# Products, differences and small sums of one transformer layer: from GpSimd to VectorE, and some sums a few matmuls later

## The chip, the cores and the metric

The kernel runs on one core of a Trainium2 chip. A core has five engines with a queue of instructions each, which they work off in order: TensorE (PE, matmuls, with its weight loads shown apart as PEld), VectorE (DVE), ScalarE (ACT), GpSimd (POOL) and SyncE (SP, which here only starts DMAs). The metric is device time in microseconds for one execution. Before the change it is 1555.61 us, the median of three runs (1555.39 to 1558.89).

## The reference, cut to what matters

The reference is one step of a one-layer streaming encoder: 1024 prompt frames and 8 short sequences of 16 frames, 1152 columns in all, model width 1024. A conditioning vector gives shifts, scales and gates for every sub-layer (adaLN). Half of the heads are a gated linear recurrence (HGRN2), the other half a latent attention (MLA) with rotary keys.

```python
def trunk_layer(x, c, pos, w, cache_lat, cache_kpe, st_hg, st_conv):
    mod = (jax.nn.silu(c) @ w_ada + b_ada)[:, None, :]
    sh1, sc1, g1, sh2, sc2, g2 = jnp.split(mod, 6, axis=-1)
    h = rmsnorm(x, g_mix) * (1.0 + sc1) + sh1
    proj = h @ w_in
    hq, hf, hi, hg, hcq, hckv, hkpe = jnp.split(proj, points, axis=-1)
    o_hg, st_hg_new = hgrn_mixer(hq, hf, hi, hg, lb, hg_g, st_hg)
    o_mla, lat_new, kpe_new = mla_mixer(hcq, hckv, hkpe, pos, ...)
    x = x + g1 * (jnp.concatenate([o_hg, o_mla], axis=-1) @ w_out)
    h2 = rmsnorm(x, g_ffn) * (1.0 + sc2) + sh2
    f, conv_new = conv_glu(h2, w_up, conv_w, conv_b, w_down, st_conv)
    return x + g2 * f, ...
```

The parts that the change touches are `h @ w_in`, the recurrence (`o` of a head is normalised with `rsqrt(mean(o * o))` and multiplied with a gain and `silu(hg)`), the rotary embedding (`x1 * cos - x2 * sin`, `x2 * cos + x1 * sin`) and the queries `rmsnorm(hcq) @ w_uq`.

## The kernel before, in words

Activations lie transposed: 128 features on the partitions, 1152 frames along the free axis, so that 1024 features are 8 tiles. A matmul in full precision is made of three: each operand is split into a rounded high part and the rest (`hi`, `lo`; `hh` and `hl` for the normalised input), and `mm3` (L291 to L295) issues hi by hi, hi by lo and lo by hi. A split is always a copy on ScalarE that rounds (`hi`), and then a subtraction of two SBUF tiles (`lo`).

The part of the program with the changed instructions goes as follows. `front` (0 to about 98 us) loads the input, makes the conditioning of the first sub-layer, normalises, and projects the first head's gates and values. Its order on TensorE, VectorE and ScalarE is the order of the code; all behind it is ordered by a scheduler, which simulates the engines with a table of costs and places each instruction on its engine's queue in the order in which it expects it to be ready. Then `phase_b` makes, for each of four heads, three units. A unit is 128 output features; `unit` (L612) runs three groups of 384 columns, and a group is 24 matmuls of 128x384 into one PSUM bank (`mm`, four banks in turn), which ScalarE copies out (L626). The weights of a unit come through `wload` (L272): DMA, high part on ScalarE (L283), low part (L284). `mla_in` (L914) goes on in the same way with five units for the latent queries and keys and one for the rotary key, and from about 430 us with the query up-projection, whose groups are 9 matmuls long; here ScalarE and then VectorE (L974, `ql`) read the PSUM bank before it is free again. Keys, scores and values of the attention follow until about 670 us, and the output projection and the channel mixer behind that; the last of the changed instructions (L905) ends at 490.6 us.

Everything else in that part is written as generators that run between the groups of main matmuls. After each group `step(n)` moves each background generator on by n pieces, and each slow one by two:

```python
    def step(self, n):
        for _ in range(n):
            self.advance(self.bg)
        for _ in range(2):
            self.advance(self.slow)
```

A piece ends at a `yield`. So a `yield` more sets what follows it behind more of the main matmuls in the program. The generators are these:
- `hgrn` (L645), the recurrence of one head: forget gate `f` and key `k` (L657, L659), seven levels of running sums and products `X` (L670 to L720) with small matmuls in L701 and L708, the products of the chunks, the state, and the output `ot`. The output is squared and split (`sq`, `sh`, `sl`, L798 to L800), summed over the partitions by matmuls with a matrix of ones (L806 for `sh`, L807 for `sl`), turned into a reciprocal root by five instructions (`rstd`, L298 to L303), and multiplied with the gate (L810, L811). With n = 4 a head's three units give it 36 pieces; the fourth head has 27 (three units with n = 3) before it is drained.
- `ada_rest` (L411), slow: the rest of the conditioning. Per pair of blocks it loads weights `wa`, multiplies (L381), copies the partial sums to SBUF on ScalarE (L390), and after a `yield` adds them up by two matmuls with a selection matrix (L394), which VectorE reads.
- In `mla_in`: `latent_q` and `latent_kv` (normalising, L833), `rope` (L850: rotated copy `rq` by DMA, products with `cos` and `sin` in L858 and L859, sum in L864), and `rope_q` (L896: splits in L903 and L905).

Names in rows: `w` are weight tiles, `X`, `Sa`, `Pa`, `k`, `f` tiles of the recurrence, `po` the outputs of units, `qr` rotary queries, `rq` their rotated copies, `u` the split up-projections of keys and values (L953, L954), `bg` PSUM banks of the background work, `s` and `t` small tiles, `c` constants.

Of the kernel before, what the change touches and what calls it, by code (L numbers as in the profile page):

```python
# [197 lines left out]
class Layer:  # L198
# [73 lines left out]
    def wload(self, src, shape, eng=None, new=None):  # L272
        nc = self.nc
        w = new or self.w
        raw, hi, lo = w(shape), w(shape, F32R), w(shape, F32R)
        nc.sync.dma_start(raw, src)
        if eng == "both":
            with self.tc.high_priority():
                nc.scalar.copy(hi, raw)
                nc.vector.tensor_sub(lo[:, :7], raw[:, :7], hi[:, :7].bitcast(F32))  # L280
                nc.gpsimd.tensor_sub(lo[:, 7:], raw[:, 7:], hi[:, 7:].bitcast(F32))
            return hi, lo
        nc.scalar.copy(hi, raw)  # L283
        (eng or nc.gpsimd).tensor_sub(lo, raw, hi.bitcast(F32))  # L284
        return hi, lo
# [100 lines left out]
    def ada_out(self, part, bs):  # L386
        nc = self.nc
        n = len(bs)
        sb = self.s([P, 256])
        nc.scalar.copy(sb, part[:, :256])  # L390
        yield
        res = self.ps("bg")
        for j in range(2):
            nc.tensor.matmul(res[:, 9 * n * j:9 * n * (j + 1)], lhsT=sb[:, P * j:P * j + P], rhs=self.sel[:, :9 * n], start=True, stop=True)  # L394
        for q, b in enumerate(bs):
            for j, (m, i) in enumerate(ADA_BLOCKS[b]):
                bias = self.vec[:, V_BADA + 8 * m + i:V_BADA + 8 * m + i + 1]
                o = self.mod[:, m, i]
                r = res[:, 9 * (n * j + q):9 * (n * j + q) + 9]
                if m in (SC1, SC2):  # L400
                    g = (V_GMIX if m == SC1 else V_GFFN) + i
                    nc.vector.tensor_scalar(o, r, bias, self.vec[:, g:g + 1], op0=ALU.add, op1=ALU.mult)
                else:
                    nc.vector.tensor_scalar_add(o, r, bias)
        yield
# [29 lines left out]
    def front(self):  # L435
# [21 lines left out]
        def stats(g):  # L457
# [3 lines left out]
            for kt in range(KT):  # L461
                if g == 0:
                    sq = l if kt == KT - 1 else self.s([P, TG])
                    nc.scalar.activation(sq, xs[kt][:, c], AF.Square)
                    if kt % 2:
                        nc.vector.tensor_add(sq, sq, pair)
                        nc.tensor.matmul(p[:, :TG], lhsT=self.ones, rhs=sq, start=kt == 1, stop=kt == KT - 1)
                    pair = sq
                else:
                    self.sumsq(l, xs[kt][:, c], kt == 0, nc.vector if g == 1 else nc.gpsimd)  # L470
                    yield
# [48 lines left out]
        with self.tc.manual_schedule(engines={mybir.EngineType.PE, mybir.EngineType.Activation, mybir.EngineType.DVE}):  # L520
# [4 lines left out]
            next(ad)  # L525
            W[0][1](nc.gpsimd, lambda: prep(0, 0))
            W[1][1](nc.vector)
            banks += [self.ps("mm") for _ in range(4)] + [self.ps("bg") for _ in range(2)]
            for kt in range(KT):
# [29 lines left out]
                if kt < 3:  # L559
                    W[kt + 2][1](nc.gpsimd if kt == 0 else nc.vector)  # L560
                if kt >= 2:
# [87 lines left out]
    def hgrn(self, hd, hf, hg, hq, v):  # L649
# [19 lines left out]
        for li, h in enumerate(LEVELS + (32,)):  # L669
# [3 lines left out]
            else:  # L673
                X = self.b(s="X")

                def vw(a, i):
                    return a[:, :ns].rearrange("p (n two h) -> p n two h", two=2, h=h)[:, :, i]
# [9 lines left out]
                if h == 1:  # L687
                    nc.gpsimd.tensor_copy(vw(X, 0), vw(k, 0))
                    nc.vector.tensor_mul(vw(X, 1), vw(hq, 1), vw(f, 1))
# [35 lines left out]
        nc.vector.tensor_mul(X[:, :, 0], X[:, :, 0], half(k, 0))  # L725
        nc.gpsimd.tensor_mul(X[:, :, 1], X[:, :, 1], half(hq, 1))
        tf = half(Pa, 0)[:, :, 63:64].to_broadcast([P, 8, 64])
# [35 lines left out]
        vb = self.b([P, 4, P], s="vb")  # L763
        nc.gpsimd.tensor_mul(vb, v[:, 8:9].to_broadcast([P, 4, P]), self.of4.unsqueeze(2).to_broadcast([P, 4, P]))
        sn = self.b([P, NB, P], s="sn")
        dec = Pa[:, SEQ:].rearrange("p (b t) -> p b t", t=DS)[:, :, DS - 1:DS].to_broadcast([P, NB, P])
        nc.gpsimd.tensor_mul(sn, s0, dec)
        pu = [self.ps("bg") for _ in range(2)]
# [17 lines left out]
        for o in range(0, NT, 4):  # L786
# [13 lines left out]
            nc.vector.tensor_sub(sl[:, c], sq[:, c], sh[:, c].bitcast(F32))  # L800
            yield
        vv, r = self.b(s="vv"), self.b(s="r")
        for o in range(0, T, TG):
# [5 lines left out]
        self.rstd(r, vv, sq)  # L809
        nc.gpsimd.tensor_mul(gate, gate, ot)  # L810
        nc.vector.tensor_mul(ot, gate, r)  # L811
# [38 lines left out]
    def rope(self, t, new):  # L850
# [6 lines left out]
        yield  # L857
        nc.gpsimd.tensor_mul(t, t, self.cos)  # L858
        nc.gpsimd.tensor_mul(q, q, self.sin)  # L859
        yield  # L860
# [34 lines left out]
    def rope_q(self, h, rr, new):  # L895
# [4 lines left out]
        a, b = self.u([P, SEQ], F32R, s="qs"), self.u([P, SEQ], F32R, s="qs")  # L900
        eng = nc.gpsimd if h else nc.vector
        nc.scalar.copy(a[:64], rr[:64, :SEQ])
# [10 lines left out]
    def mla_in(self):  # L913
# [24 lines left out]
        for n, u in enumerate(order):  # L938
            if n % 2 == 0:
# [4 lines left out]
                nc.scalar.copy(hi, raw)  # L944
                nc.gpsimd.tensor_sub(lo, raw, hi.bitcast(F32))
                for i, j in enumerate(pr):
# [280 lines left out]
    def sumsq(self, acc, x, first, eng=None):  # L1227
        nc = self.nc
        eng = eng or nc.gpsimd
        if first:  # L1230
# [424 lines left out]
```

## Time and profile before

| | |
|---|---|
| Median of three runs | 1555.61 us |
| The profiled execution's own time | 1556.36 us |
| Its span | 1554.5 us |
| Mean granted clock of TensorE | 0.983 |
| PE busy | 1489.3 us, 96% |
| DVE busy | 974.1 us, 63% |
| ACT busy | 690.5 us, 44% |
| POOL busy | 225.7 us, 15% |

The span begins with the first instruction that the profiler records and ends with the last; the execution's own time is 1.86 us longer. An engine is busy from the start of an instruction to its end, also where it is held up inside it. Rows of waits say which engine and line waited for which, how long in total, how often, and the longest; rows of the timeline say when an instruction began and how long it, or several merged ones (x3), took. The granted clock of TensorE is 1.00 at 2.4 GHz and 0.50 at 1.2 GHz.

### The profile page before, as it was taken

The numbers are of one execution on the slowest core, as the hardware profiler recorded it, in microseconds if no ns is written. First come the engines' busy times: TensorE is split into PE (matmuls) and PEld (weight loads), VectorE is DVE, ScalarE is ACT, GpSimd is POOL, SyncE is SP. The second block draws the span as 40 slices with busy tenths as digits, with TensorE's granted clock in tenths as the row PEclk, the third lists the DMA queues.
The fourth block names the chain that finished last, engine by engine and source line by source line (L and its number), as shares of the span: only waits on it lengthen the run. The fifth ranks groups of instructions, "written<-read, shape, count | busy, mean of one in ns | idle before, by whom it ended". The sixth has DMA issues, their size and how long they took to land.

```text
span 1554.5 us, 28456 instructions
## 1 busy us (share of the span) xinstructions
PE 1489.3 (96%) x11756; PEld 1386.5 (89%) x11756; DVE 974.1 (63%) x1540; ACT 690.5 (44%) x1231; POOL 225.7 (15%) x217
## 2 busy tenths in 40 slices
PE   6999999999999999998699999999999999999997
PEld 4897778998998978698699999999999999999997
DVE  5677667476777656358776655665666554473384
ACT  4453435263546646336554443443444443343352
POOL 1122232333242000012300000000000000000020
PEclk8999999999999999999899999999999999999999
DMA  9234622112131356744112211221122288455360
GB/s 345 87 109 141 217 89 106 43 72 74 50 93 26 109 192 213 285 162 165 56 56 72 85 70 67 77 85 71 58 85 83 72 279 294 154 177 199 102 250 29
DMA packets 71922, 194.42 MB, mean 125 GB/s; under 512 B 8112, under 2 KB 30384, under 8 KB 71792
## 3 DMA queue, kind: packets, MB, share of 16 engines
q1 hardware_dynamic: 60624, 165.62, 30.8%
q10 hardware_dynamic: 11168, 26.98, 4.5%
q8 instruction: 92, 1.51, 0.4%
q14 instruction: 38, 0.31, 0.1%
HBM read 159.63 MB, written 31.17 MB: 123 GB/s over the span
## 4 chain that ended last, share of the span: by engine, by line
PE 85%; DVE 7%; ACT 3%; issue 2%; DMA 2%; POOL 1%; SPq 0%; ACTq 0%; DVEq 0%; POOLq 0%
PE mm L1453 18%; PE bg L1453 13%; PE mm L293 11%; PE mm L294 11%; PE mm L295 11%; PE bg L294 3%; PE bg L295 3%; PE bg L293 3%; PE bg L1139 2%; PE bg L381 1%; PE bg L708 1%; PE bg L1182 1%; DVE sl L800 1%; DMA wa<-in_w_ada 1%; PE bg L791 1%
## 5 line engine op out<-in xcount | busy, mean ns | idle before, releaser
L1453 PE MATMUL mm<-U,W 128*128 128x288 f32 x1848 | 260.8, 296 | 11.5 <-ACT U L288 9.6
L1453 PEld LDWEIGHTS mm<-U,W 128*128 128x128 f32 x1848 | 251.5, 189 | 13.3 <-ACT U L288 9.8
L1453 PE MATMUL bg<-U,W 128*128 128x288 f32 x1320 | 189.3, 297 | 0.0
L1453 PEld LDWEIGHTS bg<-U,W 128*128 128x128 f32 x1320 | 181.7, 190 | 0.3
L289 DVE TENSOR_TENSOR W<-B,W 128x512 fp32r<-128x512 f32 (+1 forms) x132 | 102.5, 780 | 106.7 <-ACT W L288 104.5
L288 ACT CAST W<-B 128x512 fp32r<-128x512 f32 (+1 forms) x132 | 91.0, 692 | 144.8 <-issue 46.8
L293 PE MATMUL mm<-hh,w 128*128 128x384 f32 x432 | 152.7, 353 | 0.0
L294 PE MATMUL mm<-hl,w 128*128 128x384 f32 x432 | 149.5, 346 | 2.0 <-DVE hl L486 2.0
L295 PE MATMUL mm<-hh,w 128*128 128x384 f32 x432 | 149.0, 345 | 0.0
L289 DVE TENSOR_TENSOR U<-W,U 128x1024 fp32r<-128x1024 f32 (+2 forms) x66 | 74.9, 1167 | 70.4 <-ACT U L288 70.3
L288 ACT CAST U<-W 128x1024 fp32r<-128x1024 f32 (+2 forms) x66 | 61.7, 972 | 87.8 <-PE mm L294 74.5
L293 PEld LDWEIGHTS mm<-hh,w 128*128 128x128 f32 x432 | 83.1, 192 | 8.2 <-issue 7.4
L293 PE MATMUL bg<-U,U 128*128 128x448 f32 (+1 forms) x264 | 90.0, 341 | 0.2 <-DVE B L1461 0.2
L294 PE MATMUL mm<-U,U 128*128 128x448 f32 (+1 forms) x264 | 89.2, 338 | 0.0
L293 PE MATMUL mm<-U,U 128*128 128x448 f32 (+1 forms) x264 | 89.2, 338 | 0.0
L295 PE MATMUL mm<-U,U 128*128 128x448 f32 (+1 forms) x264 | 89.2, 338 | 0.0
L295 PE MATMUL bg<-U,U 128*128 128x448 f32 (+1 forms) x264 | 89.2, 338 | 0.0
L294 PE MATMUL bg<-U,U 128*128 128x448 f32 (+1 forms) x264 | 89.2, 338 | 0.0
L1456 ACT COPY B<-mm 128x288 f32<-128x288 f32 x132 | 51.8, 393 | 82.0 <-PE mm L1453 66.0
L294 PEld LDWEIGHTS mm<-hl,w 128*128 128x128 f32 x432 | 83.4, 193 | 3.5 <-DVE hl L486 2.3
L295 PEld LDWEIGHTS mm<-hh,w 128*128 128x128 f32 x432 | 83.3, 193 | 0.8 <-issue 0.8
L293 PE MATMUL mm<-mh,W 128*128 128x288 f32 x256 | 77.0, 302 | 5.5 <-DVE x L1372 3.4
(405 smaller groups left out, 3343.8 us busy)
## 6 DMA issues: line engine op xcount, KB each, us to landing
wa<-in_w_ada SPq DMA_DIRECT2D x48, 512.0 KB, 6.9
B<-in_w_up SPq DMA_DIRECT2D x44, 512.0 KB, 3.2
W<-in_w_down SPq DMA_DIRECT2D x44, 512.0 KB, 4.6
gd<-B ACTq DMA_DIRECT2D x22, 576.0 KB, 2.8
B<-in_w_down SPq DMA_DIRECT2D x22, 512.0 KB, 3.3
w<-in_w_in SPq DMA_DIRECT2D x18, 512.0 KB, 3.5
lT<-in_latT SPq DMA_DIRECT2D x16, 512.0 KB, 8.0
ln<-in_lat SPq DMA_DIRECT2D x16, 512.0 KB, 6.0
```

The source lines that it names most:

```text
L288: self.nc.scalar.copy(hi, raw)
L289: self.nc.vector.tensor_sub(lo, raw, hi.bitcast(F32))
L293: mm(out, lhsT=w[0], rhs=x[0], start=start, stop=False)
L294: mm(out, lhsT=w[0], rhs=x[1], start=False, stop=False)
L295: mm(out, lhsT=w[1], rhs=x[0], start=False, stop=stop)
L381: self.nc.tensor.matmul(part[32 * j:32 * j + 32, :256], lhsT=sc[:, 4 * half + j], rhs=w[half][:, j], start=first and half == 0, stop=last ...
L708: nc.tensor.matmul(pb[c:c + 32, 32 * j:32 * j + 32], lhsT=xl[:, o:o + 32], rhs=xr[:, o:o + 32], start=True, stop=True, tile_position=(0, c))
L791: nc.tensor.matmul(pb[:, c], lhsT=v[:, j], rhs=AF_[:, j], start=True, stop=j == 0)
L800: nc.vector.tensor_sub(sl[:, c], sq[:, c], sh[:, c].bitcast(F32))
L1139: mm(d[64 * j:64 * j + 64, :w], lhsT=q, rhs=ks[j][c], start=c == 0, stop=c == 2, tile_position=(0, 64 * j))
L1453: nc.tensor.matmul(out, lhsT=l[:, k], rhs=x[:, k], start=start and k == 0 and i == 0, stop=stop and k == 3 and i == 2, skip_group_check=True)
L1456: nc.scalar.copy(t[:, h], X[h][:, :HALF])
```

## The change

Fourteen kinds of instructions change their engine, and two places get more `yield`s.

From GpSimd to VectorE go: the low part of the unit weights (L284, 17 of 128x1024) and of two weights in `front` (L454), the sums of squares over the third group of columns (L470 and L1235, 7 of 128x384), one product `X` of each head (L726, 128x512), `vb` and `sn` of each head (L764 128x512, L767 128x1024), the gate product of each head (L810, 128x1152), both rotary products (L858 and L859, 6 of 128x1152), the splits of two rotary queries (L903, L905, 2 of 64x1024), and the low part of the query up-projection weights (L945, 3 of 128x768). One copy per head (L688, 128x576) goes from GpSimd to ScalarE. The matmuls of the sums L806 and L807 come three pieces later, and those of L394 one piece later when they are for two blocks. GpSimd keeps 157 of 214 rows of its program, VectorE has 1541 in place of 1481; TensorE has the same matmuls. Lines from L394 on have numbers higher by 2 after the change, those from L806 on by 4.

```diff
--- before.py
+++ after.py
@@ -281,7 +281,7 @@
                 nc.gpsimd.tensor_sub(lo[:, 7:], raw[:, 7:], hi[:, 7:].bitcast(F32))
             return hi, lo
         nc.scalar.copy(hi, raw)
-        (eng or nc.gpsimd).tensor_sub(lo, raw, hi.bitcast(F32))
+        nc.vector.tensor_sub(lo, raw, hi.bitcast(F32))
         return hi, lo
 
     def split(self, hi, lo, raw):
@@ -389,6 +389,8 @@
         sb = self.s([P, 256])
         nc.scalar.copy(sb, part[:, :256])
         yield
+        if len(bs) > 1:
+            yield
         res = self.ps("bg")
         for j in range(2):
             nc.tensor.matmul(res[:, 9 * n * j:9 * n * (j + 1)], lhsT=sb[:, P * j:P * j + P], rhs=self.sel[:, :9 * n], start=True, stop=True)
@@ -467,7 +469,7 @@
                         nc.tensor.matmul(p[:, :TG], lhsT=self.ones, rhs=sq, start=kt == 1, stop=kt == KT - 1)
                     pair = sq
                 else:
-                    self.sumsq(l, xs[kt][:, c], kt == 0, nc.vector if g == 1 else nc.gpsimd)
+                    self.sumsq(l, xs[kt][:, c], kt == 0, nc.vector)
                     yield
             if g:
                 nc.tensor.matmul(p[:, :TG], lhsT=self.ones, rhs=l, start=True, stop=True)
@@ -523,7 +525,7 @@
             ad = self.ada(0, wa[0])
             next(ad)
             next(ad)
-            W[0][1](nc.gpsimd, lambda: prep(0, 0))
+            W[0][1](nc.vector, lambda: prep(0, 0))
             W[1][1](nc.vector)
             banks += [self.ps("mm") for _ in range(4)] + [self.ps("bg") for _ in range(2)]
             for kt in range(KT):
@@ -557,7 +559,7 @@
                 if kt + 1 < KT:
                     prep(kt + 1, 0)
                 if kt < 3:
-                    W[kt + 2][1](nc.gpsimd if kt == 0 else nc.vector)
+                    W[kt + 2][1](nc.vector)
                 if kt >= 2:
                     for _ in range(4):
                         next(early, 0)
@@ -685,7 +687,7 @@
                 nc.vector.tensor_add(vw(Sa, 0), vw(Sa, 0), ts)
                 nc.vector.tensor_add(vw(Pa, 1), vw(Pa, 1), tf)
                 if h == 1:
-                    nc.gpsimd.tensor_copy(vw(X, 0), vw(k, 0))
+                    nc.scalar.copy(vw(X, 0), vw(k, 0))
                     nc.vector.tensor_mul(vw(X, 1), vw(hq, 1), vw(f, 1))
                 else:
                     nc.vector.tensor_mul(vw(X, 0), vw(X, 0), vw(k, 0))
@@ -723,7 +725,7 @@
         nc.scalar.activation(X[:, :, 0], half(Sa, 0), AF.Exp)
         nc.scalar.activation(X[:, :, 1], half(Pa, 1), AF.Exp)
         nc.vector.tensor_mul(X[:, :, 0], X[:, :, 0], half(k, 0))
-        nc.gpsimd.tensor_mul(X[:, :, 1], X[:, :, 1], half(hq, 1))
+        nc.vector.tensor_mul(X[:, :, 1], X[:, :, 1], half(hq, 1))
         tf = half(Pa, 0)[:, :, 63:64].to_broadcast([P, 8, 64])
         ts = half(Pa, 1)[:, :, 63:64].to_broadcast([P, 8, 64])
         nc.vector.tensor_add(half(Sa, 0), half(Sa, 0), ts)
@@ -761,10 +763,10 @@
                     nc.vector.scalar_tensor_tensor(S[:, j], S[:, j - 1], Pa[:, P * j + P - 1:P * j + P], u, op0=ALU.mult, op1=ALU.add)
         nc.scalar.dma_start(self.O["sp_o"][hd], S[:, 7])
         vb = self.b([P, 4, P], s="vb")
-        nc.gpsimd.tensor_mul(vb, v[:, 8:9].to_broadcast([P, 4, P]), self.of4.unsqueeze(2).to_broadcast([P, 4, P]))
+        nc.vector.tensor_mul(vb, v[:, 8:9].to_broadcast([P, 4, P]), self.of4.unsqueeze(2).to_broadcast([P, 4, P]))
         sn = self.b([P, NB, P], s="sn")
         dec = Pa[:, SEQ:].rearrange("p (b t) -> p b t", t=DS)[:, :, DS - 1:DS].to_broadcast([P, NB, P])
-        nc.gpsimd.tensor_mul(sn, s0, dec)
+        nc.vector.tensor_mul(sn, s0, dec)
         pu = [self.ps("bg") for _ in range(2)]
         for i in range(2):
             c = slice(64 * i, 64 * i + 64)
@@ -799,6 +801,8 @@
             nc.scalar.copy(sh[:, c], sq[:, c])
             nc.vector.tensor_sub(sl[:, c], sq[:, c], sh[:, c].bitcast(F32))
             yield
+        for _ in range(3):
+            yield
         vv, r = self.b(s="vv"), self.b(s="r")
         for o in range(0, T, TG):
             c = slice(o, o + TG)
@@ -807,7 +811,7 @@
             nc.tensor.matmul(p, lhsT=self.ones_r, rhs=sl[:, c], start=False, stop=True)
             nc.vector.tensor_scalar(vv[:, c], p, 1.0 / P, EPS, op0=ALU.mult, op1=ALU.add)
         self.rstd(r, vv, sq)
-        nc.gpsimd.tensor_mul(gate, gate, ot)
+        nc.vector.tensor_mul(gate, gate, ot)
         nc.vector.tensor_mul(ot, gate, r)
         nc.scalar.dma_start(self.mix[hd], ot)
         yield
@@ -855,8 +859,8 @@
             nc.sync.dma_start(q[d:d + 32], t[e:e + 32])
         yield
         yield
-        nc.gpsimd.tensor_mul(t, t, self.cos)
-        nc.gpsimd.tensor_mul(q, q, self.sin)
+        nc.vector.tensor_mul(t, t, self.cos)
+        nc.vector.tensor_mul(q, q, self.sin)
         yield
         yield
         yield
@@ -898,7 +902,7 @@
         yield
         yield
         a, b = self.u([P, SEQ], F32R, s="qs"), self.u([P, SEQ], F32R, s="qs")
-        eng = nc.gpsimd if h else nc.vector
+        eng = nc.vector
         nc.scalar.copy(a[:64], rr[:64, :SEQ])
         eng.tensor_sub(a[64:], rr[:64, :SEQ], a[:64].bitcast(F32))
         nc.scalar.copy(b[64:], rr[64:, :SEQ])
@@ -942,7 +946,7 @@
                 for i, j in enumerate(pr):
                     nc.sync.dma_start(raw[:, i], I["w_uq"][:, j])
                 nc.scalar.copy(hi, raw)
-                nc.gpsimd.tensor_sub(lo, raw, hi.bitcast(F32))
+                nc.vector.tensor_sub(lo, raw, hi.bitcast(F32))
                 for i, j in enumerate(pr):
                     wq[j] = (hi[:, i], lo[:, i])
             if n == 3:
@@ -1226,7 +1230,7 @@
 
     def sumsq(self, acc, x, first, eng=None):
         nc = self.nc
-        eng = eng or nc.gpsimd
+        eng = eng or nc.vector
         if first:
             nc.scalar.activation(acc, x, AF.Square)
         else:
```

The scheduler then orders all queues anew, and three places of its result are shown here.

On TensorE, in the group of main matmuls in which the third head's output is summed (`mm` are the main matmuls, `bg` the sums of `sh` and `sl`), before the change:

```order
L806 MATMUL bg_3579<-sh_3539,c_76 128x384
L294 MATMUL mm_3602<-hl_113,w_2986 128x384
L806 MATMUL bg_3583<-sh_3539,c_76 128x384
L295 MATMUL mm_3602<-hh_112,w_2987 128x384
L807 MATMUL bg_3579<-sl_3540,c_76 128x384
L807 MATMUL bg_3583<-sl_3540,c_76 128x384
L293 MATMUL mm_3602<-hh_114,w_2986 128x384
```

and after it (L810 and L811 are the former L806 and L807):

```order
L295 MATMUL mm_3580<-hh_122,w_2987 128x384
L810 MATMUL bg_3608<-sh_3539,c_76 128x384
L811 MATMUL bg_3608<-sl_3540,c_76 128x384
L810 MATMUL bg_3612<-sh_3539,c_76 128x384
L811 MATMUL bg_3612<-sl_3540,c_76 128x384
L810 MATMUL bg_3616<-sh_3539,c_76 128x384
L811 MATMUL bg_3616<-sl_3540,c_76 128x384
L293 MATMUL mm_3628<-hh_108,w_2986 128x384
```

All six sums now stand together behind the whole group of 24 main matmuls, where before they began ahead of it, right behind the products of the head's output.

On TensorE, in the second head, where the sums of the conditioning (L394) stand among the main matmuls and the small matmuls of the levels (L708), before:

```order
L708 MATMUL bg_2184<-X_2177 32x32 x36
L708 MATMUL bg_2229<-X_2222 32x32 x36
L381 MATMUL bg_2138<-wa_2147,c_74 32x256 x4
L381 MATMUL bg_2138<-wa_2148,c_74 32x256 x4
L293 MATMUL mm_2291<-hh_108,w_1779 128x384
L294 MATMUL mm_2291<-hl_109,w_1779 128x384
L295 MATMUL mm_2291<-hh_108,w_1780 128x384
L293 MATMUL mm_2291<-hh_110,w_1779 128x384
L394 MATMUL bg_2277<-c_70,s_2275 128x18 x2
L294 MATMUL mm_2291<-hl_111,w_1779 128x384
```

and after:

```order
L381 MATMUL bg_2104<-wa_2113,c_74 32x256 x4
L381 MATMUL bg_2104<-wa_2114,c_74 32x256 x4
L293 MATMUL mm_2250<-hh_108,w_1740 128x384
L294 MATMUL mm_2250<-hl_109,w_1740 128x384
L295 MATMUL mm_2250<-hh_108,w_1741 128x384
L293 MATMUL mm_2250<-hh_110,w_1740 128x384
L294 MATMUL mm_2250<-hl_111,w_1740 128x384
L295 MATMUL mm_2250<-hh_110,w_1741 128x384
L710 MATMUL bg_2195<-X_2188 32x32 x36
L293 MATMUL mm_2250<-hh_112,w_1740 128x384
```

The sum that belongs to these two rows of L381 stood four main matmuls behind them; it now stands 32 behind them, with L710 (the former L708) of two levels and L703 of the next in between. The L708 of a head, which stood in pairs, stand apart among the main matmuls.

On VectorE, in the query up-projection, before the change (L974 are the subtractions that free the PSUM bank `mm` named in them):

```order
L974 TENSOR_TENSOR ql_4798<-mm_4812,qh_4797 128x384
L954 TENSOR_TENSOR u_4845<-w_4843,u_4844 128x1024
L974 TENSOR_TENSOR ql_4798<-mm_4830,qh_4797 128x256
L954 TENSOR_TENSOR u_4851<-w_4849,u_4850 128x1024
L864 TENSOR_TENSOR po_4581<-po_4581,rq_4715 128x1152
L974 TENSOR_TENSOR ql_4856<-mm_4857,qh_4855 128x384
L974 TENSOR_TENSOR ql_4856<-mm_4870,qh_4855 128x384
L974 TENSOR_TENSOR ql_4856<-mm_4882,qh_4855 128x256
L289 TENSOR_TENSOR kl_4826<-po_4581,kh_4825 128x1024
L974 TENSOR_TENSOR ql_4903<-mm_4904,qh_4902 128x384
L974 TENSOR_TENSOR ql_4903<-mm_4926,qh_4902 128x384
L864 TENSOR_TENSOR qr_4703<-qr_4703,rq_4758 128x1152
```

and after (L978, L958, L868 are the former L974, L954, L864, and L862 and L863 the rotary products):

```order
L978 TENSOR_TENSOR ql_4798<-mm_4812,qh_4797 128x384
L862 TENSOR_TENSOR po_4581<-po_4581,cos_4376 128x1152
L863 TENSOR_TENSOR rq_4715<-rq_4715,sin_4377 128x1152
L978 TENSOR_TENSOR ql_4798<-mm_4830,qh_4797 128x256
L868 TENSOR_TENSOR po_4581<-po_4581,rq_4715 128x1152
L958 TENSOR_TENSOR u_4845<-w_4843,u_4844 128x1024
L958 TENSOR_TENSOR u_4851<-w_4849,u_4850 128x1024
L862 TENSOR_TENSOR qr_4703<-qr_4703,cos_4376 128x1152
L863 TENSOR_TENSOR rq_4758<-rq_4758,sin_4377 128x1152
L289 TENSOR_TENSOR kl_4826<-po_4581,kh_4825 128x1024
L978 TENSOR_TENSOR ql_4856<-mm_4857,qh_4855 128x384
L868 TENSOR_TENSOR qr_4703<-qr_4703,rq_4758 128x1152
```

Between the subtraction on `mm_4812` and the one on `mm_4857` stood four instructions; nine stand there now, four of them rotary products, and one the split of the rotary key (L289).

## Rows read from the trace of the kernel before

**Rows 1.** Busy time by stretch: stretch, its length, busy us of each engine, clock, DMA.

```profile
0.00:60.00 60.00, 45.58 (x303) 33.19 (x304) 36.52 (x76) 28.23 (x56) 11.46 (x13) 0.87 0.75 278
60.00:215.00 155.00, 148.44 (x1875) 131.81 (x1874) 106.41 (x197) 71.66 (x130) 40.02 (x23) 0.97 0.40 135
215.00:545.00 330.00, 316.87 (x2889) 292.84 (x2890) 223.00 (x366) 157.73 (x321) 88.80 (x48) 0.99 0.21 70
545.00:1554.00 1009.00, 978.39 (x6693) 928.63 (x6689) 608.15 (x902) 432.83 (x725) 85.41 (x135) 0.99 0.38 133
```

**Rows 2.** Waits of TensorE, whole span: total us, times, longest us.

```profile
PE bg L807 <- DVE sl L800: 5.9, 4, 1.6
PE bg L394 <- ACT s L390: 5.3, 6, 2.0
...
PE mm L1047 <- ACT w L1024: 3.4, 2, 3.1
PE mm L293 <- DVE ql L974: 3.1, 1, 3.1
...
PE mm L294 <- DVE hl L486: 2.0, 1, 2.0
...
PE bg L311 <- DVE acc L840: 1.1, 1, 1.1
PE bg L701 <- DVE X L692: 1.1, 1, 1.1
PE bg L708 <- DVE k L659: 1.0, 1, 1.0
```

**Rows 3.** Waits of TensorE from 0 to 60 us, those of L394 alone.

```profile
PE bg L394 <- ACT s L390: 2.0, 4, 0.5
```

**Rows 4.** Busy time in three stretches at half clock (columns as in Rows 1).

```profile
57.80:61.20 3.40, 3.28 (x11) 3.28 (x12) 3.40 (x5) 1.76 (x4) 2.13 (x2) 0.50 0.00 0
201.20:208.00 6.80, 6.67 (x22) 6.67 (x23) 6.05 (x12) 1.33 (x3) 2.75 (x1) 0.50 0.80 272
457.20:460.60 3.40, 3.40 (x13) 3.40 (x11) 2.90 (x5) 2.06 (x5) 1.64 (x1) 0.51 0.43 92
```

**Rows 5.** Timeline of GpSimd and VectorE, 230 to 235 us: start, us, instruction.

```profile
232.77 2.66 POOL L810 TENSOR_TENSOR gate<-gate,ot 128x1152 f32<-128x1152 f32 x1 [1.36 <-ACT ot L796]
...
231.43 0.69 DVE L800 TENSOR_TENSOR sl<-sq,sh 128x512 fp32r<-128x512 f32 x1 [3.85 <-ACT sh L799]
...
233.24 2.74 DVE L800 TENSOR_TENSOR sl<-sq,sh 128x512 fp32r<-128x512 f32 x1
```

**Rows 6.** Timeline of GpSimd and VectorE, 53.5 to 58 us.

```profile
55.17 3.55 POOL L1235 TENSOR_TENSOR s<-s,s 128x384 f32<-128x384 f32 x3 [0.34 <-ACT s L1234]
...
53.88 3.98 DVE L486 SCALAR_TENSOR_TENSOR hl<-x,c,hh 128x384 fp32r<-128x384 f32 x3
```

**Rows 7.** Timeline of VectorE, 384 to 403 us, the fourth head's reciprocal root.

```profile
393.12 3.45 DVE L303 SCALAR_TENSOR_TENSOR r<-sq,r 128x1152 f32<-128x1152 f32 x1
```

**Rows 8.** Groups of VectorE by shape: busy us, mean ns of one.

```profile
L289 DVE TENSOR_TENSOR W<-B,W 128x1024 fp32r<-128x1024 f32 x22 | 26.8, 1219 | 2.1 <-ACT W L288 2.1
...
L811 DVE TENSOR_TENSOR ot<-gate,r 128x1152 f32<-128x1152 f32 x4 | 5.4, 1357 | 0.3
```

**Rows 9.** Timeline of VectorE, 444 to 458 us, the query up-projection.

```profile
446.32 0.56 DVE L974 TENSOR_TENSOR ql<-mm,qh 128x384 fp32r<-128x384 f32 x1 [0.98 <-ACT qh L973]
...
449.25 3.36 DVE L954 TENSOR_TENSOR u<-w,u 128x1024 fp32r<-128x1024 f32 x1
452.53 3.79 DVE L864 TENSOR_TENSOR po<-po,rq 128x1152 f32<-128x1152 f32 x1
456.25 1.34 DVE L974 TENSOR_TENSOR ql<-mm,qh 128x384 fp32r<-128x384 f32 x3
```

**Rows 10.** Timeline of VectorE, 482 to 490 us, the first softmax.

```profile
485.90 2.24 DVE L1019 TENSOR_TENSOR t<-t,t 128x1 f32<-128x1 f32 x1
```

**Rows 11.** Waits of GpSimd, whole span, those of L284.

```profile
POOL w L284 <- ACT w L283: 188.4, 15, 32.5
```

## The prediction

> **What bounds the kernel now.** I read the busy times by stretch first [rows 1]. TensorE is busy 1489.3 of 1554.0 us, so a change that leaves its matmuls alone can act only on its idle time and on its clock. Of the 64.7 us that the four rows leave idle, 30.6 lie behind 545 us, where no changed instruction is, and 14.4 in the first 60 us, most of it waits for the first loads, which stay. What remains is 6.6 us between 60 and 215 and 13.1 us between 215 and 545. The waits of TensorE [rows 2] give those 20 us names. L807 waits four times for the low part of the squares (5.9 us), L394 for a copy of ScalarE (5.3 us, of which four short ones, 2.0 us, stand in the start [rows 3], in code that the change does not reorder, so 3.3 count: one of 2.0 and one of 1.3), then single waits of 3.1 (`ql`), 3.1 (L1047), 2.0 (`hl`), 1.1 (L311), 1.1 (L701) and 1.0 us (L708).
>
> Then the clock. Three stretches of the heads and the start run at the 1.2 GHz level [rows 4], and each begins some 2 to 4 us behind one of the longer waits: 57.8 behind the wait for `hl` (it ended at 55.9), 201.2 behind L394's 2.0 us (199.3), 457.2 behind the wait for `ql` (453.7). At half speed a stretch costs half its length: 1.7, 3.4 and 1.7 us. The waits of L807, at most 1.6 us, have none behind them.
>
> Last I looked at why VectorE is late at these places. Alone, a subtraction of 128x512 takes 0.69 us; beside GpSimd's gate product, which takes 2.66, the same one takes 2.74 and ends with it [rows 5]. Three `hl` beside the sums of squares take 3.98 us [rows 6], 1.33 each. L303 (128x1152) takes 3.45 [rows 7] where such an instruction takes 1.36 [rows 8], L954 3.36 and L864 3.79 [rows 9], a subtraction of single columns 2.24 [rows 10]. So VectorE stands still while GpSimd reads its tiles.
>
> The Trainium skill says this in "SBUF — State Buffer", section "Who interferes with whom": a VectorE instruction with two SBUF inputs shares a read port with GpSimd, and the one that comes second is blocked entirely, not slowed. The trace agrees (0.69 against 2.74 us beside the 2.66 of L810). Taken alone, that rule would make each meeting pair cheaper on VectorE (0.69 + 1.36 against 2.74), and each pair that does not meet dearer by the whole moved instruction; which of the two prevails is decided by the sums below.
>
> **What VectorE takes over.** Its durations go with the columns: 0.69 for 512, 1.22 for 1024, 1.36 for 1152 [rows 5, 8], so about 0.56 for 384 and 0.95 for 768 by the line through them. That makes 17 + 2 + 4 + 2 of 1024 (30.5 us), 4 + 6 of 1152 (13.6), 4 + 4 of 512 (5.5), 7 of 384 (3.9), 3 of 768 (2.9): 56 us more work. What it gets back is the blocking, and for five of the examples above alone that is 2.05 (L800), 2.1 (L303), 2.1 (L954), 2.4 (L864) and 2.3 us (three `hl`); I estimate 40 us in all before 545 us, since GpSimd reads there for some 127 us and VectorE is busy two thirds of the time. The net is some 15 us on an engine that is idle for a third of those stretches [rows 1]; by itself it costs nothing, and what counts is where it stands in the queue. The copy L688 on ScalarE (four, under 0.8 us each, with ScalarE busy 46 to 48% there [rows 1]) I take at 0, between -0.5 and +1 each.
>
> **Place by place**, in us of TensorE's time:
>
> 1. The wait for `hl` at 55.9. GpSimd's sums are gone, `hl` takes its own time, and the sums go to VectorE behind `prep`, where it has gaps. The wait goes (-2.0) and the clock stays up (-1.7): **-3.7**, between -4 and 0.
> 2. First head. L394 stands a group later, so its copy is long done (-1.3); L807 comes behind 24 main matmuls of 0.175 us, 4.2 us, against a wait of 1.0, what 5.9 leaves beside three of up to 1.6 [rows 2] (-1.0). L701 waits for products on VectorE that were held up by L284 on GpSimd; now L284 itself is in that queue behind L283, and I leave its 1.1 us. A transpose that waits for `Sa` gets later by about 0.5. **-1.8**, between -3.4 and +2.
> 3. Second head. L394 goes with its half-clock stretch (-2.0 - 3.4), L708's first wait goes (-1.0). But the small matmuls of the levels now stand apart, and VectorE's chain between two of them, four products of 0.7 us and the copy out of PSUM, gets an L284 of 1.22 in between at three levels. Followed through the new order with the durations above, three waits of 0.95, 0.55 and 0.9 come in (+2.4). **-4.0**, between -6.4 and +1.
> 4. L807 in the second, third and fourth head: 5.9 - 1.0 = 4.9 goes, since 24 main matmuls cover it each time; +0.5 for the copy L688 ahead of an exponential in the fourth. **-4.4**, between -4.9 and -2.
> 5. L311 at 400.8. The fourth head has 27 pieces for its generator, whose number of yields goes from 24 to 27: the end of its chain moves as far back as it can. Six instructions of 1.36 (root, gate, and the sums of the latent norm) then end about 0.9 later against what TensorE wants, though L303 loses its 2.1 of blocking. **+0.9**, between -1.1 and +4 (with half clock).
> 6. `ql` at 453.7. The L974 ahead ended at 446.9, and the one that frees the bank at 456.8 [rows 9]; between them stood two L954, L864 and a subtraction of 0.4. Now four rotary products of 1.36, L868 1.36, two of 1.22, the key's split of 1.22 and the 0.4 stand there, 10.9 us, so with its own 0.56 it ends at 458.3. The wait grows by 1.5, its half-clock stretch by some 0.5: **+2.0**, between -4.9 (wait and stretch gone) and +4.
> 7. L1047 at 486. L1019 loses its blocking (2.24 to 0.15), and a copy of ScalarE for the rotary query then comes last. **-1.0**, between -3.1 and +1.
>
> Sum: -3.7 - 1.8 - 4.0 - 4.4 + 0.9 + 2.0 - 1.0 = -12.0. The profiled execution took 1556.36, its span 1554.5 and 1.86 around it; the median is 0.75 below. 1556.4 - 12.0 = 1544.4, against the median's level 1543.6: I say **1544**. The bounds added up are -23.8 and +10.
>
> **The rivals.** (a) *Everything goes.* VectorE is idle a third of the time, so my three new waits of the second head (2.4), the 0.9 at L311 and the waits of `ql` (3.1 and 1.7 of clock) and L1047 (3.1) may all go. That is 2.4 + 2.0 (0.9 and the old 1.1) + 6.8 (2.0 and 4.8) + 2.1 = 13.3 beyond the forecast: 1531. For it speaks that the blocked instructions were the last ahead of all these waits; against it that the new queue at the `ql` place holds more than the old one, blocked time included.
>
> (b) *No difference.* The heads are paced by VectorE's chain and not by the waits that TensorE shows: what is saved at L394 and L807 comes back at the next L708, as a stalled chain with 15 us more work in it. Then the heads' -1.8 - 4.0 - 4.4 fall away, and -3.7 + 0.9 + 2.0 - 1.0 = -1.8 is left: 1554. For it: TensorE's total wait is small against its busy time, so the schedule already was tight; against: TensorE is ahead only where main matmuls run out between two small ones, and there are 24 more in front of each moved sum.
>
> (c) *Slower: L284 blocks VectorE's queue.* GpSimd waited 188.4 us in 15 pieces, up to 32.5, for ScalarE's L283 [rows 11], which waits for TensorE to give weight buffers free. On GpSimd nothing stood behind it; on VectorE the whole chain of a head does, and the scheduler places L284 by its own costs. If L283 comes later than planned by 2 us, L708 or a PSUM bank does too. The price is the wait of 2 us and a half-clock stretch of 1.7, as at 55.9: 3.7 a time. From four of the 17 onward the gain is gone; with seven, 26 - 12 = +14, it is 1569. Against it: those long waits show that L283's end was far behind GpSimd's, not that it is uncertain.
>
> By a sentence of the Trainium skill ("Perfetto Trace Analysis", section "Optimizing Scalar/DVE Operations") work is moved away from VectorE when that engine is saturated, and a move between it and GpSimd might not help since they share a port. VectorE has no such stretch here: the fullest of rows 1 has 69%.
>
> **How the numbers follow.** The forecast has 0.62, (a) 0.12, (b) 0.16, (c) 0.10. About 0.3%, 4.7 us, is what a measurement of this kernel can tell from no change. The forecast's own range is 1537 to 1551, all of it faster; (b) is inside the 4.7 us, (c) outside above. Faster 0.74, within 0.3% 0.16, slower 0.10. The range of 8 in 10 reaches from 1533, near (a), to 1556, which takes in (b).
>
> **What would show it.** The half-clock stretches behind 55.9 and 199.3 should be gone, and TensorE's waits for `sl` and for the copy L390 from the second 60 us on. The wait for `ql` should stay, at 4 to 5 us, with its stretch. L800 should take 0.7 throughout, and L303 1.36. VectorE's busy time should rise by 10 to 20 us, that of GpSimd fall by some 125. The forecast is wrong if new waits above 2 us stand at L710 or L703 (the former L708 and L701) in two heads or more, or if TensorE waits for VectorE behind an L284 that itself waits for L283.

## The result, and the profile after

The changed kernel takes 1536.51 us (median of four runs, 1533.27 to 1539.24), the kernel before beside it 1557.25: a ratio of 0.9879 with a 95% interval of 0.9856 to 0.9901, that is 15 to 22 us less. Forecast were 12 us less, 1544. The time lies in the range of 8 in 10 (1533 to 1556) and just below the forecast's own 1537 to 1551, about midway between the forecast and rival (a)'s 1531: the size was too small.

The profiled execution of the changed kernel is the longest of the four (1539.24 us, span 1537.5). Its busy line on the page:

```profile
PE 1481.9 (96%) x11756; PEld 1381.8 (90%) x11756; DVE 979.6 (64%) x1593; ACT 694.5 (45%) x1235; POOL 99.2 (6%) x160
```

GpSimd loses 126.5 us of busy time, VectorE gains 5.5 in place of the 10 to 20 that I gave it: it did some 56 us more work and stood still some 50 us less, where I had estimated 40. TensorE's waits between 60 and 525 us, where those that the prediction took from [rows 2] for this part are 18.6 us:

```profile
PE mm L293 <- DVE ql L978: 3.8, 1, 3.8
PE bg L381 <- DMA wa<-in_w_ada: 2.4, 2, 1.8
PE mm L1051 <- ACT w L1028: 1.8, 2, 1.5
PE mm L1051 <- DVE Vl L1010: 0.9, 1, 0.9
PE bg L1071 <- DVE t L1023: 0.7, 1, 0.7
...
```

No wait for `sl`, for the copy L390, for `X`, `k` or `acc` is left. VectorE in the second head's output and in the fourth head's root (start, us):

```profile
215.87 1.35 DVE L814 TENSOR_TENSOR gate<-gate,ot 128x1152 f32<-128x1152 f32 x1
217.14 0.89 DVE L802 TENSOR_TENSOR sl<-sq,sh 128x512 fp32r<-128x512 f32 x2
...
375.63 1.36 DVE L303 SCALAR_TENSOR_TENSOR r<-sq,r 128x1152 f32<-128x1152 f32 x1
```

L802, the former L800, is 0.68 us for 512 columns (0.89 with the 128 behind it) right behind the gate product, against 2.74 in [rows 5]; L303 takes 1.36 against 3.45 in [rows 7]. VectorE in the query up-projection:

```profile
429.39 2.35 DVE L958 TENSOR_TENSOR u<-w,u 128x1024 fp32r<-128x1024 f32 x2
431.66 1.35 DVE L862 TENSOR_TENSOR qr<-qr,cos 128x1152 f32<-128x1152 f32 x1
432.93 1.35 DVE L863 TENSOR_TENSOR rq<-rq,sin 128x1152 f32<-128x1152 f32 x1
434.20 1.22 DVE L289 TENSOR_TENSOR kl<-po,kh 128x1024 fp32r<-128x1024 f32 x1
435.33 0.55 DVE L978 TENSOR_TENSOR ql<-mm,qh 128x384 fp32r<-128x384 f32 x1
```

Each is as short as alone, and still L978 comes last: the queue is long now, where it was blocked in [rows 9]. The half-clock stretches of the heads (stretch, length, busy, clock):

```profile
127.80:131.20 3.40, 3.40 (x17) 2.15 (x16) 2.44 (x2) 1.25 (x2) 0.00 (x0) 0.51 0.02 5
435.00:441.80 6.80, 5.86 (x18) 5.87 (x19) 6.41 (x9) 2.72 (x4) 0.93 (x4) 0.50 0.01 2
```

The columns are those of Rows 1. The stretches of [rows 4] at 57.8 and 201.2 are gone, the third is twice as long, and a new one follows a wait of L381 (1.8 us, until 126.8).

### The profile page after: what moved, and what is told of

It is laid out like the page before. It is cut to its first block, busy times and chain, and to the rows that moved or that the text cites. A ratio compares the mean times of both kernels' runs of the same rounds, so it can differ in the third digit from the quotient of the medians.

```text
span 1537.5 us, 28393 instructions
## 1 busy us (share of the span) xinstructions
PE 1481.9 (96%) x11756; PEld 1381.8 (90%) x11756; DVE 979.6 (64%) x1593; ACT 694.5 (45%) x1235; POOL 99.2 (6%) x160
## 4 chain that ended last, share of the span: by engine, by line
PE 87%; DVE 5%; DMA 2%; ACT 2%; issue 2%; POOL 1%; SPq 0%; ACTq 0%; DVEq 0%; POOLq 0%
PE mm L1457 17%; PE bg L1457 13%; PE mm L293 11%; PE mm L295 11%; PE mm L294 11%; PE bg L294 4%; PE bg L293 4%; PE bg L295 4%; PE bg L1143 2%; PE bg L381 1%; DMA wa<-in_w_ada 1%; PE bg L1186 1%; PE bg L710 1%; DVE U L289 1%; PE bg L793 1%
## 5 line engine op out<-in xcount | busy, mean ns | idle before, releaser
L289 DVE TENSOR_TENSOR W<-B,W 128x512 fp32r<-128x512 f32 (+1 forms) x132 | 102.5, 779 | 107.8 <-ACT W L288 105.5
L293 PE MATMUL mm<-hh,w 128*128 128x384 f32 x432 | 150.8, 349 | 0.0
L295 PE MATMUL mm<-hh,w 128*128 128x384 f32 x432 | 147.5, 341 | 0.0
L289 DVE TENSOR_TENSOR U<-W,U 128x1024 fp32r<-128x1024 f32 (+2 forms) x66 | 74.8, 1166 | 72.1 <-ACT U L288 68.3
```

The source lines that it names most:

```text
L289: self.nc.vector.tensor_sub(lo, raw, hi.bitcast(F32))
L293: mm(out, lhsT=w[0], rhs=x[0], start=start, stop=False)
L295: mm(out, lhsT=w[1], rhs=x[0], start=False, stop=stop)
```

## The experiments

All were timed against the kernel before in five rounds. A ratio is the time of the version to that of the kernel before beside it, with its 95% interval in brackets; the gain in us follows from it. Waits and timelines are those of one profiled execution each. Theory 1 is the prediction's: GpSimd blocks VectorE, and the later sums cover what is left.

**The later sums alone**: only the two additional `yield`s of the diff.

> The kernel before with the additional yields alone; every product stays on GpSimd. Theory 1 (both halves of the change work: GpSimd no longer blocks VectorE, and the later sums cover what is left): L807's waits (5.9 us) and L394's (1.4 and 2.0 us, with the half-clock stretch behind the second, 3.4) go, the wait for hl (2.0, stretch 1.7) and the one for ql (3.1) stay, and L303 blocked at 3.45 us makes the wait at L311 longer by about 1: some 11 us faster, 1546. Theory 2 (the later sums carry all, the engines matter at hl alone): 16 us faster, 1541, with VectorE still blocked beside GpSimd. Theory 3 (the engines carry all, the sums came late only since VectorE was blocked): under 5 us, 1553.

The ratio is 0.9958 (0.9941 to 0.9974), 6.5 us. L807's and L394's waits go, though the longest L802 still takes 2.78 us. But L381 waits for its weights now:

```profile
PE bg L381 <- DMA wa<-in_w_ada: 7.3, 2, 4.8
```

Of the expected 11 us 4.5 are missing. These 7.3 us, a new wait of 1.8 for `X` at L710 and two half-clock stretches behind the waits of L381 (6.8 and 3.4 us in this execution) are more than that; the waits at L701 and L708, gone as well, work the other way. So the missing time has several causes, and they were not tried one by one.

**The engines alone**: the changed kernel without the additional `yield`s.

> The changed kernel without the additional yields. Theory 1: hl goes with its stretch (3.7), L807's waits shrink to under 0.5 each (L800 takes 0.69 in place of 2.7 us; 4.5 of 5.9 go), L311 loses 1; L394's 3.4 us of waits and its stretch of 3.4 stay, since a copy of ScalarE is waited for there; ql gets 2 worse: some 7 us faster, 1550. Theory 2: 4 us faster, from hl alone, 1553. Theory 3: 18 to 20 us faster, as the whole change, 1538.

The ratio is 0.9909 (0.9891 to 0.9927), 14.1 us: twice theory 1's 7, about three quarters of the whole, and short of theory 3's 18 to 20. L807 waits nowhere. The row on which theory 1 falls is L394's, whose two waits of 3.4 us shrink to this without its `yield`:

```profile
PE bg L394 <- ACT s L390: 0.5, 1, 0.5
```

**The sums of squares alone**

```diff
-                    self.sumsq(l, xs[kt][:, c], kt == 0, nc.vector if g == 1 else nc.gpsimd)
+                    self.sumsq(l, xs[kt][:, c], kt == 0, nc.vector)
```

> The kernel before with one line changed: the sums of squares of the third group of columns are made on VectorE. The order on TensorE is the same. Theory 1: three hl take 1.8 us in place of 3.98, the wait of 2.0 us at 55.9 and the half-clock stretch behind it (1.7) go: 3.7 us faster, 1553.5, and nothing else in the trace moves. Rival: the seven sums of 0.56 us each stand in VectorE's queue ahead of the next hl, and a wait of the same size comes back at a later one before 98 us: no difference.

The ratio is 0.9985 (0.9973 to 0.9997), 2.3 us. The wait for `hl` goes and does not come back before 100 us. The interval, 0.5 to 4.2 us, holds theory 1's 3.7 and only just leaves out the rival's nothing.

**The gate product alone**

```diff
-        nc.gpsimd.tensor_mul(gate, gate, ot)
+        nc.vector.tensor_mul(gate, gate, ot)
```

> The kernel before with one line changed: the gate product of each head (L810) is made on VectorE. Theory 1: the four blocked L800 take 0.69 us in place of 2.7, the gate product takes 1.36 ahead of them, and L807's waits fall from 5.9 us to under 2: some 4 us faster, 1553. Rival (a queue for a port): the gate product stands ahead of L800 on VectorE, so that L800 ends only 0.7 us earlier than before and L807's waits fall by 4 x 0.7 at most: under 3 us, not to be told from no change.

The ratio is 0.9943 (0.9927 to 0.9958), 8.9 us, more than either theory. All four waits of L807 are gone (5.9 us), where theory 1 left up to 2: the scheduler, which now sees the gate product in VectorE's queue, itself sets the last two L807 of a head 4 to 6 main matmuls later. What the other 3 us are is not settled; in this execution L394's wait of 2.0 us is also down to 0.6, and no half-clock stretch stands between 61 and 753 us.

**The low parts of the weights alone**

```diff
-        (eng or nc.gpsimd).tensor_sub(lo, raw, hi.bitcast(F32))
+        nc.vector.tensor_sub(lo, raw, hi.bitcast(F32))
```

> The kernel before with one line changed: the low parts of the unit weights (L284, 17 of 128x1024) are made on VectorE. No sum comes later. Theory 1b (the waits that the profile puts down to the copy L390, and the one for X, are GpSimd's L284 blocking VectorE: before, L691 took 2.52 us beside it, L686 ended at 200.3, ScalarE's exponential L684 waited 2.2 for it, and L390 stood behind that): L394's waits of 1.4 and 2.0 us and L701's of 1.1 go, L807's 5.9 stay: 4.5 us faster, up to 3.4 more where a half-clock stretch followed, 1549 to 1551. Rival (c) of the prediction (L284 in VectorE's queue, waiting for ScalarE's L283, holds up the heads): waits of 2 us or more at L708 or L701 in two heads, no faster than before, 1555 to 1560. Rival 2 (L394 waits since it stands too early in the program): its waits stay, under 2 us faster.

The ratio is 0.9977 (0.9965 to 0.9989), 3.6 us. Of TensorE's waits from 60 to 545 us:

```profile
PE bg L807 <- DVE sl L800: 5.8, 4, 1.6
...
PE bg L394 <- ACT s L390: 0.7, 1, 0.7
PE bg L701 <- DVE X L692: 0.4, 1, 0.4
```

L394 falls from 3.4 to 0.7, L701 from 1.1 to 0.4, L807 stays: theory 1b. No L691 takes more than 0.76 us, where the longest before took 2.53. No wait of L708 or L701 is above 0.7, so L284 in VectorE's queue delays no head; rival (c) of the prediction is wrong. The three moves tried alone add up to 14.8 us, beside 14.1 for all engines together. If gains simply add, the moves that were not tried alone (L688, L726, L764, L767 and others) bring nothing that these intervals could show.

**The rotary products back on GpSimd**

```diff
-        nc.vector.tensor_mul(t, t, self.cos)
-        nc.vector.tensor_mul(q, q, self.sin)
+        nc.gpsimd.tensor_mul(t, t, self.cos)
+        nc.gpsimd.tensor_mul(q, q, self.sin)
```

> The changed kernel with the rotary products (six of 128x1152) back on GpSimd. Theory 1: VectorE's queue in the query up-projection is 5.4 us shorter, but the two splits and the rotary sum there are blocked again (about 3.3 and 3.7 us in place of 1.2 and 1.4): the wait for ql falls from 3.8 to 3.1, and the wait at L1051 goes from 1.5 back to 3.1: 1 us slower than the changed kernel, 1537 to 1538. Rival (the rotary products are what VectorE had no room for): the wait for ql goes with the stretch behind it, 4 to 7 us faster than the changed kernel, 1530 to 1532.

The ratio is 0.9879 (0.9859 to 0.9899), beside 0.9867 (0.9846 to 0.9889) of the changed kernel on the same chip: no difference. The rival is out, and theory 1's 1 us is too little to be told from none; its two waits did not come as it said. The one at L1051 stayed at 1.5, and the one for `ql` did not fall but rose to 4.7, since VectorE is blocked three times ahead of it:

```profile
424.62 3.29 DVE L958 TENSOR_TENSOR u<-w,u 128x1024 fp32r<-128x1024 f32 x1 [0.39 <-ACT u L957]
...
428.17 3.37 DVE L958 TENSOR_TENSOR u<-w,u 128x1024 fp32r<-128x1024 f32 x1
431.46 3.76 DVE L868 TENSOR_TENSOR po<-po,rq 128x1152 f32<-128x1152 f32 x1
435.14 1.01 DVE L978 TENSOR_TENSOR ql<-mm,qh 128x384 fp32r<-128x384 f32 x2
```

**The rotary part later**, on the changed kernel:

```diff
         nc = self.nc
+        for _ in range(0 if h else 3):
+            yield
         yield from self.rope(rr, new)
...
-                    nc.vector.tensor_sub(lo[:, c], p[:, :m], hi[:, c].bitcast(F32))
+                    with self.tc.high_priority():
+                        nc.vector.tensor_sub(lo[:, c], p[:, :m], hi[:, c].bitcast(F32))
```

> The changed kernel with two edits for the wait for ql: the rotary part of the first two query heads starts three pieces later, and the subtraction that frees a PSUM bank (L978) gets priority in the scheduler, so that five instructions in place of nine stand between those on mm_4810 and mm_4857. Theory 1: 4 x 1.2 to 1.4 and 0.4 us stand there, the bank is free before TensorE wants it, the wait of 3.8 us goes with the stretch behind it (1.7 to 3.4): 4 to 7 us faster than the changed kernel, 1530 to 1533. Rival: the same wait comes back as one for the next bank or for the rotary queries at the first scores (L1051): no difference from the changed kernel, 1536.

The ratio is 0.9836 (0.9813 to 0.9859), the median 1530.41: the fastest kernel of this study, 4.6 us under the changed one beside it (the intervals overlap a little). Which of the two edits does it was not tried. Its longest wait from 60 to 520 us is now

```profile
PE mm L1054 <- ACT w L1031: 1.8, 2, 1.5
```

and no wait for `ql` is among them. Its profiled execution has no half-clock stretch between 30 and 736 us.

**The change again**

> The changed kernel as it is, beside the others on the same chip. Both theories: the ratio to before of the first measurement, 0.988, 1537; the waits in the profile are the same, and the half-clock stretches need not stand where they stood.

The ratio is 0.9867 (0.9846 to 0.9889), as the first time.

**No `yield` ahead of L394**, once on the changed kernel, once on the version with the later rotary part; the three ahead of L806 stay.

> The changed kernel without the additional yield ahead of L394; the three yields ahead of L806 stay. Theory 1b (L394's copy was late because ScalarE waited for a blocked VectorE; the yield only holds the conditioning's weight buffers longer, so that L381 waits for wa, 2.4 us in the changed kernel's profile, 7.3 where the later sums were tried alone): L394's waits do not come back, L381's fall under 1 us: 1 to 3 us faster than the changed kernel, 0.986 of before, 1533. Rival (the prediction's step: L394 must stand a group later): waits of 1.3 and 2.0 us at L394 again, some 3 us slower, 0.990, 1539.

> The version with the later rotary part and the prior L978, without the yield ahead of L394. Theory 1b: as above on top of that version, 1 to 2 us under its 0.9836 of before: 0.983, 1528. Rival: 3 us over it, 0.986, 1533.

The ratios are 0.9911 (0.9897 to 0.9926) and 0.9871 (0.9854 to 0.9887): 5 to 7 us slower than with it, both times, though L394 waits no more than 0.5 and 0.7 us and L381 not at all. Both were timed on another chip than the change again and the later rotary part, each beside the kernel before, and the intervals just meet in two of the three comparisons; the two results and the profiles below agree. So both theories fail: the waits behave as 1b says, the time as the rival says. Two things follow. Between the engines with the three `yield`s (0.9911) and the engines alone (0.9909) there is no difference that intervals of 2 to 3 us on either side could show. And the one `yield` ahead of L394 is worth some 5 us without a wait. A part can be seen in the second head. L771 (L773 in the changed kernel) is two pairs of matmuls, each on one half of the rows of the array. Without the `yield` nine main matmuls stand between the pairs:

```profile
210.88 1.09 PE L771 MATMUL bg<-vb,kn 64*128 64x512 f32 x2
...
213.69 1.12 PE L771 MATMUL bg<-vb,kn 64*128 64x512 f32 x2
```

In the changed kernel they are neighbours, and the four take as long as two:

```profile
205.61 1.13 PE L773 MATMUL bg<-vb,kn 64*128 64x512 f32 x4
```

That is 1.1 us. The other part is that TensorE changes between main and background matmuls more often. Without the `yield`:

```profile
205.01 0.34 PE L295 MATMUL mm<-hh,w 128*128 128x384 f32 x1
205.19 0.34 PE L293 MATMUL mm<-hh,w 128*128 128x384 f32 x1
205.45 0.64 PE L381 MATMUL bg<-wa,c 128*32 128x256 f32 x8
206.02 0.44 PE L294 MATMUL mm<-hl,w 128*128 128x384 f32 x1
206.30 0.34 PE L295 MATMUL mm<-hh,w 128*128 128x384 f32 x1
```

In the changed kernel:

```profile
208.23 1.48 PE L381 MATMUL bg<-wa,c 128*32 128x256 f32 x24
209.63 0.44 PE L294 MATMUL mm<-hl,w 128*128 128x384 f32 x1
```

From start to start a main matmul takes 0.18 us ahead of another one, but 0.26 ahead of L381 and 0.28 as the first one behind it; eight L381 between main matmuls take 0.57, and 24 in a row 1.40, that is 0.47 for eight. From about 70 us to the query up-projection TensorE goes from main to background matmuls and back 67 times without the `yield` and 59 times with it. There, counted from the start of each matmul to the start of the next and with waits left out, the 1512 main matmuls take 1.7 us less with the `yield`, L771 1.0, L381 0.8, L708 0.5 and L748 0.2: 4.2 us together, against 0.2 to 0.6 us more of waits. This compares the two profiles without the `yield` with those of the change again and of the later rotary part, which have no half-clock stretch there either. It accounts for most of the 5 us; it is read from the profiles and was not tried by itself.

## Why the prediction was right, and where it was too small

**What held.** Most of the gain is idle time of TensorE in the first 545 us, and the waits go because VectorE is no longer blocked. `hl`: -3.7 was the term, and between the 97th and the 145th of the matmuls of `mm3` the two profiles differ by 3.7; alone it measured 2.3. `ql`: +2.0 was the term, with a wait that stays; it is 0.6 longer, its stretch 3.4 longer, 1.8 us by the same matmuls ahead and behind. L1047: -1.0 was the term; its wait halved, and two new ones (0.9 and 0.7) took that back, about 0. Rivals (b) and (c) are out. Rival (a) held for the three new waits of the second head and for L311, 4.4 of its 13.3 us, and failed at `ql` and L1047.

**Two steps failed.** The first is "L394 stands a group later, so its copy is long done". The waits go without it, so that the term for these waits (-1.3 and -2.0) came out right by luck. The chain in the kernel before was this, GpSimd and VectorE, then ScalarE:

```profile
196.82 2.38 POOL L284 TENSOR_TENSOR w<-w,w 128x1024 fp32r<-128x1024 f32 x1 [12.54 <-ACT w L283]
197.22 2.52 DVE L691 TENSOR_TENSOR X<-X,k 128x512 f32<-128x512 f32 x1
199.67 0.68 DVE L686 TENSOR_TENSOR Pa<-Pa 128x512 f32<-128x512 f32 x1
```

```profile
200.38 0.63 ACT L684 ACTIVATE X<-Pa 128x512 f32<-128x512 f32 x1 [2.22 <-DVE Pa L686]
200.92 0.35 ACT L390 COPY s<-bg 128x256 f32<-128x256 f32 x1
```

L284 on GpSimd blocks L691, which ends only 0.5 us behind it (199.7 and 199.2), so L686 is late, ScalarE's L684 waits 2.22 us for it, and L390 stands behind L684. The row of waits names only the last link, ScalarE. The low parts alone show it: with L284 on VectorE and no `yield` more, both the long L691 and L394's waits are gone.

The second is the premise that a change which leaves TensorE's matmuls alone "can act only on its idle time and on its clock". It also acts on their order, which the prediction put at nothing: by starts of matmuls, the same ones took 4.3 us less in the heads, and the last experiment shows 4.2 us from one `yield` that saves no wait.

**Terms that were too small.** The heads and L311 were -1.8 - 4.0 - 4.4 + 0.9 = -9.3: -5.9 of waits and -3.4 of half clock. The first matmul of the query up-projection starts 21.5 us earlier than before (411.4 against 432.9); 2.0 of them come from the start, where the execution before happened to have a longer half-clock stretch, 3.7 are `hl`, and 15.8 are the heads. Of these 15.8, waits are 9.8, half clock 1.7 and the closer matmuls 4.3, above all the sums L806 and L807 that now stand together (1.7), L381 (1.6), L755 and L771 (0.7 each). In the waits, the three new ones of the second head (+2.4) and two later arrivals (+0.5 each) never came, and no run shows why; L311 (+0.9) lost its wait of 1.1 instead, with L303 back at 1.36; L701's 1.1, which I left standing, went with L284. Against that stand 2.4 us of new waits of L381, which no step of mine had. The half clock gave back less than 3.4 since a new stretch of 3.4 us, which costs 1.7, follows one of these waits. Without the closer matmuls the time would have come out within some 3 us of the forecast: the larger part of what was missing is a cause that the prediction had ruled out.

Two readings of the prediction were wrong. 55.9, 199.3 and 453.7 are where the three waits began, not where they ended; TensorE went on at 57.9, 201.3 and 456.9, so each half-clock stretch begins within 0.4 us of the end of its wait. And the lower bounds of the seven places add up to -27.8, not -23.8.

**L807** came out right (-5.9) for a cause that was there twice: the later sums remove it with VectorE still blocked, the gate product on VectorE removes it without the three `yield`s.

## What to carry to other kernels

A wait names its last releaser; follow that engine's queue back to the first instruction that took longer than the same shape takes elsewhere. Where one engine blocks another, work moved to the faster of them can cost less than its own duration: 56 us of work moved here and 5.5 us of busy time more. And a `yield` that only moves work re-orders everything behind it: time such an edit alone before crediting it with the wait that it was meant for, and count how often TensorE changes between two kinds of matmuls.

## What the runs showed of the hardware that was not expected

A wait does not fix the half-clock stretch behind it. The same wait for `ql`, 3.1 to 3.2 us, has one of 3.4 us behind it in the profiles of before, of the later sums and of the low parts, one of 6.8 in that of the squares, and none in that of the gate product; the versions with the later rotary part, which do not wait for `ql`, have none there either. The wait of 2.0 us for `hl` has none in that of the low parts, and L394's, 2.1 us in that of the squares, none there. I had counted such stretches as fixed prices of 1.7 to 3.4 us; they differ from one execution to the next, and runs of one kernel differ by several us.

Matmuls on different halves of the array's rows ran side by side only as neighbours: 1.13 us for two pairs, 1.09 and 1.12 for each by itself.

Changing between main matmuls and L381 cost TensorE time without any wait: 0.26 and 0.28 us in place of 0.18 for the main matmuls on either side.
